# Two-block network on one core: the second block's projections in another order, its convolution without GpSimd

## The chip, the cores and the metric

One core of a Trainium2 chip runs the whole network in one program, everything in 32 bits. The figure is the device's time for the program in microseconds, the median of three runs.

## The reference

Two blocks follow each other on 256 tokens of 2048 channels, each two layers deep. The change is in the second block. It puts 16 learned tokens ahead (272 in all), normalizes, and runs this layer twice:

```
proj = h @ w_in                      # 2048 -> 5120 columns, nine segments
(c_val, c_glu, c_gate, q, k, v, a_gate, r_x, r_gate) = split(proj)

c = c_val * sigmoid(c_glu)                         # convolution branch, 512 channels
c = causal_depthwise_conv(c, conv_dw_w, conv_dw_b) # 31 taps
c = silu(layer_norm(c)) @ conv_pw_w + conv_pw_b
y_conv = c * silu(c_gate)

q, k = partial_rotary(q), partial_rotary(k)        # 16 query heads, 4 key heads of 64
y_attn = sliding_window_sink_attention(q, k, v, sinks) * silu(a_gate)

r = rg_lru(causal_depthwise_conv(r_x, lru_conv_w)) # recurrence over the tokens, 512 channels
y_lru = r * silu(r_gate)

h = layer_norm(alpha * h + concat(y_conv, y_attn, y_lru) @ w_out)
```

## The kernel before

**Weights stream past the operand.** Every product is done in three matmuls of half the precision each: a weight and the operand are split into a high part, a rounding, and a low part, the remainder. `weights` (L67) brings a half of a weight unit, 128x1024, by SP's DMA queue, ACT rounds it to `hi` (L76), and DVE subtracts to get `lo` (L78); there are three buffers for the raw half and four each for `hi` and `lo`. Such a half unit is the beat of the program: `wstat` (L103) does the 24 matmuls of a half unit (L119 to L121) into one of two sums in PSUM, `acc`, and then calls `tick` (L59). A projection of 512 columns is eight half units; its two sums are handed to an eviction at the end of half units six and eight.

**Side work is generators.** What is not a projection (attention, the convolution, the recurrence) is written as Python generators. `spawn` (L50) runs the first step of one, and every `tick` runs one step of each that is alive. This sets when the instructions are issued in the program, in half units. A planner then orders the instructions of each engine: it walks a model of the engines, takes what is ready, and among that what was issued first. `high_priority(offset=n)` makes instructions count as issued n instructions earlier, and a negative offset later: weights are 400 ahead, the convolution's taps 400 behind (`CONV_LATER`). The order of each engine is fixed in the program.

**A layer of block 2** (`layer`, L1093) does ten projections of the same normed operand `ht`: keys and values first, two of queries, then the convolution's value and gate, the recurrence's input, two gates of attention, the recurrence's gate and the convolution's gate. Then comes the pointwise product of the convolution (two half units, `pointwise`, L843), and four projections out of the four gated branches `ys`.

- The first projection runs before the layer norm of its operand is known. It is made of rows about a shift; `normed_acc` (L758) corrects it: the columns' mean part is scaled on ACT from `delta`, subtracted from PSUM on DVE (L766), multiplied by `rs` (L767), and shifted on ACT.
- `conv_branch` (L792) goes through 62 steps spread over 24 half units (`CONV_TICKS`). In each, DVE does one tap of a channel chunk (multiply and add, L790), and the side path does one of another chunk: ACT scales (L787), GpSimd adds (L788). Then come the layer norm over 512 channels, with sums on GpSimd and matmuls, and the split of the result, in eleven half units.
- `attend_kv` (L974) handles four heads that share keys, in 14 steps; the four of them start six half units apart.
- `lru_branch` (L865) does 16 taps on DVE with the same helper `tap` (L778), then gates, exponentials and a scan.
- `evict_k` and `evict_v` (L925, L937) rotate the keys, copy them for each head on GpSimd, and turn the values.
- In block 1, `layer_tables` (L174) loads constants and gains by GpSimd's DMA queue, pinned in the order of the program.

Of the kernel before, what the change touches and what calls it, by code (L numbers as in the profile page):

```python
# [35 lines left out]
class Net:  # L36
# [12 lines left out]
    # side work is a generator; the weight stream advances each by a step per half unit  # L49
# [32 lines left out]
    # tokens on the PSUM partitions: 512 columns of a weight, two token blocks  # L82
# [18 lines left out]
    # channels on the PSUM partitions: two subgroups of 256 columns. Where both parts of x fit  # L101
    # a bank, one matmul takes both, and the sums are added at the end
# [41 lines left out]
class Block1(Net):  # L144
# [29 lines left out]
    def layer_tables(self, l):  # L174
        nc, a, cp, cst = self.nc, self.a, self.tp, self.cst
        tabs = []
        load = lambda out, src: self.tc.keep_in_program_order(nc.gpsimd.dma_start(out=out, in_=src))
# [34 lines left out]
    # two channel chunks of x -> gained, split operand  # L212
# [185 lines left out]
    # two heads; st holds what the weight stream has brought  # L398
# [74 lines left out]
    # four heads  # L473
# [109 lines left out]
CONV_TICKS = 24  # L583
# [13 lines left out]
# columns of the per-channel parameters of a layer  # L597
CW, CB, CG, CBB, PB, LW, LB, BA, BX, LAM, PG, PBT, N_PC = 0, 124, 128, 132, 136, 140, 156, 160, 164, 168, 172, 188, 204
ROTC, ROTS, BAND, MCAUS, N_CST2 = 0, L2, 2 * L2, 2 * L2 + 416, 2 * L2 + 416 + 16
SHUFFLE = list(range(8, 16)) + list(range(0, 8)) + list(range(16, 32))  # L600


class Block2(Net):
# [18 lines left out]
    # layer norm over the channels, which lie on the partitions: sums about a shift. With gb, the  # L622
    # rows about the shift, times g, and g and b as two more columns, are an operand by themselves
# [112 lines left out]
    # the rows of hx, normed; their operand takes the place of the one about the shift, block by  # L736
    # block, when the first projection has read that
# [19 lines left out]
    # W g (x - shift) with W g and W b as further columns -> W applied to the normed rows  # L757
    def normed_acc(self, acc):  # L758
        nc = self.nc
        w = self.sm.tile([P, 2, 2], F32, tag="wgb", bufs=2, name="w")  # L760
        t = self.s2()
        with self.tc.high_priority(offset=GATE):
            nc.vector.tensor_copy(w, acc[:, :, L2 : L2 + 2])
            for c in range(2):
                nc.scalar.activation(t[:, c, :], self.delta, AF.Copy, scale=w[:, c, 0:1])
            nc.vector.tensor_tensor(out=t, in0=acc[:, :, :L2], in1=t, op=ALU.subtract)  # L766
        nc.vector.tensor_tensor(out=t, in0=t, in1=bc(self.rs, [P, 2, L2], 1), op=ALU.mult)  # L767
        for c in range(2):
            nc.scalar.activation(t[:, c, :], t[:, c, :], AF.Identity, bias=w[:, c, 1:2])
        return t  # L770
# [7 lines left out]
    def tap(self, pad, wbase, k, bias, out, c, j, side=False):  # L778
# [6 lines left out]
        elif side:  # L785
            t = self.cv.tile([P, L2], F32, tag="tap", bufs=4, name="tap")
            nc.scalar.activation(t, x, AF.Copy, scale=w)  # L787
            nc.gpsimd.tensor_tensor(out=o, in0=o, in1=t, op=ALU.add)  # L788
        else:
            nc.vector.scalar_tensor_tensor(out=o, in0=x, scalar=w, in1=o, op0=ALU.mult, op1=ALU.add)  # L790

    def conv_branch(self, cpad, res):  # L792
        nc = self.nc
        y = self.cv.tile([P, 4, L2], F32, tag="cv", name="y")
        for j in range(2 * TAPS):
            with self.tc.high_priority(offset=-CONV_LATER):
                self.tap(cpad, CW, TAPS, CB, y, j // TAPS, j % TAPS)
                self.tap(cpad, CW, TAPS, CB, y, 2 + j % 2, j // 2, side=True)
# [126 lines left out]
    def evict_k(self, acc):  # L925
        nc = self.nc
        t = self.normed_acc(acc)
# [8 lines left out]

    def evict_v(self, acc):  # L937
        nc = self.nc
        t = self.normed_acc(acc)
# [33 lines left out]
    # four heads that share keys  # L973
# [119 lines left out]
    def layer(self, l, gb_in):  # L1093
# [25 lines left out]
        wst(0, lambda sg, acc: self.spawn(self.evict_v(acc)) if sg else self.evict_k(acc), n=L2 + 2)  # L1119
        while norm in self.gens:  # L1120
            self.tick()
        self.spawn(self.decay())
        qq = self.Tp.tile([P, 2, 4, L2], F32, tag="T", name="qq")

        def attention():
# [278 lines left out]
```

## Time and profile before

| | |
|---|---|
| median of three runs | 3346.55 us |
| lowest, highest | 3342.49, 3347.16 us |
| span of the profiled execution | 3344.8 us |
| PE busy | 3272.3 us (98%) |
| DVE busy | 2204.3 us (66%) |
| ACT busy | 1653.2 us (49%) |
| GpSimd busy | 396.0 us (12%) |

PE is the matmul engine, PEld its load of weights, DVE the vector engine, ACT the scalar engine, POOL GpSimd, SP the engine whose queue issues the DMAs. The span goes from the first to the last instruction of one execution; it lies between the lowest and the highest of the three times. A busy PE is not PE at its peak, so the number of matmuls in a stretch says more than its busy time. Block 1 ends and block 2 begins at about 2490 us; its second layer begins at about 2915.

### The profile page before, as it was taken

How to read it: one execution, taken by the hardware profiler on the slowest of the kernel's cores; microseconds unless marked ns; L12 is line 12 of the kernel's file. 1: busy time of each engine (PE TensorE's matmuls, PEld its weight loads, DVE VectorE, ACT ScalarE, POOL GpSimd, SP SyncE). 2: the span in 40 equal slices, each digit the busy share in tenths (PEclk: the TensorE clock that was granted, in tenths of full speed). 3: DMA queues.
4: the chain of work that ended last, by engine and by line, in shares of the span. 5: the costliest groups of instructions: out<-in, count | busy, mean ns of one | idle time of the engine just before them, and what ended most of it. 6: DMA issues, size and time to landing. Idle time of an engine off the chain costs nothing.

```text
span 3344.8 us, 48525 instructions
## 1 busy us (share of the span) xinstructions
PE 3272.3 (98%) x19138; PEld 2878.7 (86%) x19138; DVE 2204.3 (66%) x2782; ACT 1653.2 (49%) x2308; POOL 396.0 (12%) x365
## 2 busy tenths in 40 slices
PE   8999999999999999999999999999999989999797
PEld 6888888888888888888888888888889989999797
DVE  7666655666665666666655666665687796776976
ACT  5444444444444454444544444444555565555653
POOL 2010100000000011110000000000032250322503
PEclk9999999999999999999999999999999999999899
DMA  6555555555555665555555555556654335453354
GB/s 217 173 170 171 172 188 188 179 176 175 174 172 187 205 212 185 171 175 169 170 193 188 178 174 174 174 176 195 199 169 155 102 125 170 158 164 103 115 181 134
DMA packets 164341, 573.05 MB, mean 171 GB/s; under 512 B 22464, under 2 KB 24768, under 8 KB 164112
## 3 DMA queue, kind: packets, MB, share of 16 engines
q1 hardware_dynamic: 163520, 567.72, 52.3%
q8 instruction: 150, 2.46, 0.3%
q0 software_dynamic: 592, 2.23, 0.2%
q14 instruction: 79, 0.65, 0.1%
HBM read 565.68 MB, written 4.19 MB: 170 GB/s over the span
## 4 chain that ended last, share of the span: by engine, by line
PE 90%; DVE 7%; issue 2%; DMA 1%; ACT 0%; POOL 0%; SPq 0%; DVEq 0%; POOLq 0%; ACTq 0%
PE acc L126 29%; PE acc L128 14%; PE acc L96 8%; PE acc L97 8%; PE acc L95 8%; PE acc L119 5%; PE acc L120 5%; PE acc L121 5%; DVE lo L78 2%; DVE y L790 2%; PE acc L125 1%; DVE x L790 1%; PE ps L343 1%; DMA raw<-wx 0%; PE ps L293 0%
## 5 line engine op out<-in xcount | busy, mean ns | idle before, releaser
L78 DVE TENSOR_TENSOR lo<-raw,hi 128x1024 fp32r<-128x1024 f32 x1060 | 1329.5, 1255 | 779.9 <-ACT hi L76 777.5
L76 ACT CAST hi<-raw 128x1024 fp32r<-128x1024 f32 x1060 | 1111.5, 1049 | 1230.6 <-PE acc L126 449.6
L126 PE MATMUL acc<-T,hi 128*128 128x512 f32 x4096 | 1439.9, 397 | 0.0
L128 PE MATMUL acc<-T,lo 128*128 128x256 f32 x3840 | 1077.7, 281 | 0.0
L126 PEld LDWEIGHTS acc<-T,hi 128*128 128x128 f32 x4096 | 762.0, 188 | 171.6
L128 PEld LDWEIGHTS acc<-T,lo 128*128 128x128 f32 x3840 | 725.8, 189 | 5.8
L119 PE MATMUL acc<-T,hi 128*128 128x272 f32 (+2 forms) x1792 | 531.1, 296 | 9.5 <-DVE t L1173 4.1
L95 PE MATMUL acc<-hi,T 128*128 128x512 f32 x1280 | 521.9, 408 | 8.6 <-ACT hi L76 8.6
L121 PE MATMUL acc<-T,lo 128*128 128x272 f32 (+2 forms) x1792 | 518.5, 289 | 2.8 <-DVE lo L78 2.8
L120 PE MATMUL acc<-T,hi 128*128 128x272 f32 (+2 forms) x1792 | 519.0, 290 | 0.9 <-POOL T L754 0.9
L96 PE MATMUL acc<-lo,T 128*128 128x512 f32 x1280 | 507.3, 396 | 3.0 <-DVE lo L78 3.0
L97 PE MATMUL acc<-hi,T 128*128 128x512 f32 x1280 | 507.0, 396 | 0.0
L119 PEld LDWEIGHTS acc<-T,hi 128*128 128x128 f32 x1792 | 344.7, 192 | 12.1 <-issue 8.0
L121 PEld LDWEIGHTS acc<-T,lo 128*128 128x128 f32 x1792 | 344.3, 192 | 3.4 <-DVE lo L78 3.4
L120 PEld LDWEIGHTS acc<-T,hi 128*128 128x128 f32 x1792 | 344.5, 192 | 2.9 <-POOL T L754 1.1
L95 PEld LDWEIGHTS acc<-hi,T 128*128 128x128 f32 x1280 | 241.6, 189 | 62.5 <-ACT hi L76 9.1
L96 PEld LDWEIGHTS acc<-lo,T 128*128 128x128 f32 x1280 | 242.3, 189 | 57.9 <-DVE lo L78 4.5
L97 PEld LDWEIGHTS acc<-hi,T 128*128 128x128 f32 x1280 | 241.3, 188 | 56.7
L133 ACT COPY sum<-acc 128x512 f32<-128x512 f32 x128 | 75.0, 586 | 222.1 <-PE acc L126 222.1
L134 DVE TENSOR_TENSOR sum<-acc,sum 128x512 f32<-128x512 f32 x128 | 88.5, 692 | 145.4 <-ACT sum L133 145.4
L788 POOL TENSOR_TENSOR y<-y,tap 128x272 f32<-128x272 f32 x120 | 123.4, 1065 | 248.7 <-ACT tap L787 129.7
L230 POOL TENSOR_TENSOR sqs<-sqs,sq 128x512 f32<-128x512 f32 x14 | 23.5, 1678 | 843.4 <-ACT sq L229 843.1
(326 smaller groups left out, 2413.8 us busy)
## 6 DMA issues: line engine op xcount, KB each, us to landing
raw<-ww SPq DMA_DIRECT2D x512, 512.0 KB, 4.3
raw<-wx SPq DMA_DIRECT2D x320, 512.0 KB, 3.8
raw<-w2in SPq DMA_DIRECT2D x160, 512.0 KB, 3.8
raw<-w2out SPq DMA_DIRECT2D x64, 512.0 KB, 4.2
x<-xT SPq DMA_DIRECT2D x8, 256.0 KB, 5.5
x<-xT SPq DMA_DIRECT2D x4, 512.0 KB, 5.9
x<-x SPq DMA_DIRECT2D x8, 256.0 KB, 3.0
x<-x SPq DMA_DIRECT2D x4, 512.0 KB, 5.1
```

Of the source, the lines that this page charges most:

```text
L76: nc.scalar.copy(hi, raw)
L78: nc.vector.tensor_tensor(out=lo, in0=raw, in1=hi.bitcast(F32), op=ALU.subtract)
L95: nc.tensor.matmul(o, xh, wh[:, k, :], start=first, stop=False)
L96: nc.tensor.matmul(o, xh, wl[:, k, :], start=False, stop=False)
L97: nc.tensor.matmul(o, xl, wh[:, k, :], start=False, stop=last)
L119: nc.tensor.matmul(o, wh[:, k, cs], xh, start=first, stop=False)
L120: nc.tensor.matmul(o, wh[:, k, cs], xl, start=False, stop=False)
L121: nc.tensor.matmul(o, wl[:, k, cs], xh, start=False, stop=last)
L126: nc.tensor.matmul(both, wh[:, k, cs], x[:, :, kc % 4, lo : lo + n], start=first, stop=last)
L128: nc.tensor.matmul(o, wl[:, k, cs], xh, start=False, stop=False)
L788: nc.gpsimd.tensor_tensor(out=o, in0=o, in1=t, op=ALU.add)
L790: nc.vector.scalar_tensor_tensor(out=o, in0=x, scalar=w, in1=o, op0=ALU.mult, op1=ALU.add)
```

## The change

Block 2's layer takes its projections in another order (the constants `CVAL` to `AGATE` give the place of each in `w2in`, which stays as it was), and the rows of `w2out` follow the new order of the branches. Value and gate of the convolution are first; then keys and values, half of the queries, the recurrence's input, the other half of the queries, the convolution's gate, the recurrence's gate, one gate of attention, the pointwise product, and the last gate of attention. The third and fourth part of attention wait until their queries are there (`there`).

The correction of the first projection is applied to the convolution's value. ACT first copies the sum out of PSUM, halved, and the correction is made on that copy and written into the convolution's input. Keys and values are copied by ACT without a correction.

The taps are spread over 44 half units. GpSimd has no part in them: ACT scales two channel chunks, and DVE adds both in one instruction (`tap_pair`), every second step. `gate` has a buffer of its own. The loads in `layer_tables` go by SP's queue and are no longer pinned, and the memory set aside for GpSimd's DMA is smaller.

```diff
-        load = lambda out, src: self.tc.keep_in_program_order(nc.gpsimd.dma_start(out=out, in_=src))
+        load = lambda out, src: nc.sync.dma_start(out=out, in_=src)
...
-CONV_TICKS = 24
+CONV_TICKS = 44
...
+CVAL, CGLU, KV, Q0, RX, CGATE, RGATE, AGATE = 3, 4, 0, 1, 5, 9, 8, 6
...
-    def normed_acc(self, acc):
+    def normed_acc(self, acc, out):
         nc = self.nc
         w = self.sm.tile([P, 2, 2], F32, tag="wgb", bufs=2, name="w")
         t = self.s2()
         with self.tc.high_priority(offset=GATE):
-            nc.vector.tensor_copy(w, acc[:, :, L2 : L2 + 2])
-            for c in range(2):
-                nc.scalar.activation(t[:, c, :], self.delta, AF.Copy, scale=w[:, c, 0:1])
-            nc.vector.tensor_tensor(out=t, in0=acc[:, :, :L2], in1=t, op=ALU.subtract)
+            nc.scalar.activation(t, acc[:, :, :L2], AF.Copy, scale=0.5)
+            nc.vector.tensor_scalar(w, acc[:, :, L2 : L2 + 2], 0.5, None, ALU.mult)
+        for c in range(2):
+            nc.vector.scalar_tensor_tensor(
+                out=t[:, c, :], in0=self.delta, scalar=w[:, c, 0:1], in1=t[:, c, :], op0=ALU.mult, op1=ALU.subtract)
         nc.vector.tensor_tensor(out=t, in0=t, in1=bc(self.rs, [P, 2, L2], 1), op=ALU.mult)
         for c in range(2):
-            nc.scalar.activation(t[:, c, :], t[:, c, :], AF.Identity, bias=w[:, c, 1:2])
-        return t
+            nc.scalar.activation(out[:, c, :], t[:, c, :], AF.Identity, scale=-1.0, bias=w[:, c, 1:2])
...
-        elif side:
-            t = self.cv.tile([P, L2], F32, tag="tap", bufs=4, name="tap")
-            nc.scalar.activation(t, x, AF.Copy, scale=w)
-            nc.gpsimd.tensor_tensor(out=o, in0=o, in1=t, op=ALU.add)
...
+    def tap_pair(self, pad, out, c, j):
+        nc = self.nc
+        t = out[:, c : c + 2, :] if j == 0 else self.cv.tile([P, 2, L2], F32, tag="tap", bufs=2, name="tap")
+        for i in range(2):
+            x, w = pad[:, c + i, j : j + L2], self.col(CW, (c + i) * TAPS + j)
+            if j == 0:
+                nc.scalar.activation(t[:, i, :], x, AF.Identity, scale=w, bias=self.col(CB, c + i))
+            else:
+                nc.scalar.activation(t[:, i, :], x, AF.Copy, scale=w)
+        if j:
+            o = out[:, c : c + 2, :]
+            nc.vector.tensor_tensor(out=o, in0=o, in1=t, op=ALU.add)
...
                 self.tap(cpad, CW, TAPS, CB, y, j // TAPS, j % TAPS)
-                self.tap(cpad, CW, TAPS, CB, y, 2 + j % 2, j // 2, side=True)
+                if j % 2 == 0:
+                    self.tap_pair(cpad, y, 2, j // 2)
...
-        t = self.normed_acc(acc)
+        t = self.taken(acc)
...
+    def taken(self, acc):
+        t = self.s2()
+        with self.tc.high_priority(offset=GATE):
+            self.nc.scalar.copy(t, acc[:, :, :L2])
+        return t
...
-        wst(0, lambda sg, acc: self.spawn(self.evict_v(acc)) if sg else self.evict_k(acc), n=L2 + 2)
+        cpad = self.cv.tile([P, 4, L2 + TAPS - 1], F32, tag="cpad", bufs=1, name="cpad")
...
+        wst(CVAL, lambda sg, acc: self.normed_acc(acc, c[:, 2 * sg : 2 * sg + 2, :]), n=L2 + 2)
         while norm in self.gens:
             self.tick()
...
+        wst(CGLU, ev)
+        self.spawn(self.conv_branch(cpad, cact))
         self.spawn(self.decay())
+        wst(KV, lambda sg, acc: self.spawn(self.evict_v(acc)) if sg else self.evict_k(acc))
...
+                while len(there) <= kv // 2:
+                    yield
...
+            wst(Q0 + cp, ev, lo)
+            there.append(cp)
+        query(0)
+        self.spawn(attention())
...
+        wst(RX, lambda sg, acc: nc.scalar.copy(rpad[:, 2 * sg : 2 * sg + 2, 3:], acc[:, :, :L2]))
         self.spawn(self.lru_branch(rpad, hlru))
+        query(1)
...
-        wst(6, gated(atts[0]), lo)
-        wst(7, gated(atts[1]), lo)
-        wst(8, gated(hlru), lo)
-        gate = self.lr.tile([P, 4, L2 + 3], F32, tag="rp", bufs=1, name="gate")
-        wst(9, lambda sg, acc: twice_silu(acc, gate[:, 2 * sg : 2 * sg + 2, lo:L2]), lo)
+        gate = self.lr.tile([P, 4, L2], F32, tag="gate", bufs=1, name="gate")
+        wst(CGATE, lambda sg, acc: twice_silu(acc, gate[:, 2 * sg : 2 * sg + 2, lo:]), lo)
+        wst(RGATE, gated(0, hlru), lo)
+        wst(AGATE, gated(2, atts[0]), lo)
         while not cact:
             self.tick()
-        ys.append(self.pointwise(a["pw"][l], cact, gate, lo))
+        ys[1] = self.pointwise(a["pw"][l], cact, gate, lo)
+        wst(AGATE + 1, gated(3, atts[1]), lo)
...
-    wo = np.concatenate([heads(wo[:, 512:1536], 1), wo[:, 1536:], wo[:, :512]], 1)
+    wo = np.concatenate([wo[:, 1536:], wo[:, :512], heads(wo[:, 512:1536], 1)], 1)
...
-    nc = bacc.Bacc("TRN2", target_bir_lowering=False, num_devices=1)
+    nc = bacc.Bacc("TRN2", target_bir_lowering=False, num_devices=1, dynamic_dma_scratch_size=1024)
```

## Rows read from the trace of the kernel before

Rows of stretches hold, in this order: the stretch in us; its length; busy time of PE, PEld, DVE, ACT and POOL, each with its number of instructions in brackets; the granted clock of the matmul engine as a share of the full one; the busy share of the DMA engines; GB/s. In rows in order of time, the bracket at the end is the idle time before the instruction and what ended it.

**Rows 1.** The profile's page: span, and engines' busy us, share, instructions:
```profile
span 3344.8 us, 48525 instructions
...
PE 3272.3 (98%) x19138; PEld 2878.7 (86%) x19138; DVE 2204.3 (66%) x2782; ACT 1653.2 (49%) x2308; POOL 396.0 (12%) x365
```

**Rows 2.** Stretches of 20 us in block 2:
```profile
2600.00:2620.00 20.00, 20.00 (x152) 18.90 (x151) 9.38 (x19) 11.23 (x27) 0.00 (x0) 1.00 0.38 123
2620.00:2640.00 20.00, 20.00 (x164) 18.87 (x164) 12.64 (x29) 8.72 (x13) 0.00 (x0) 1.00 0.32 106
...
2660.00:2680.00 20.00, 18.04 (x117) 17.24 (x115) 20.00 (x23) 13.31 (x25) 20.00 (x20) 0.83 0.24 79
2680.00:2700.00 20.00, 13.64 (x102) 12.82 (x102) 20.00 (x23) 14.71 (x29) 20.00 (x21) 0.89 0.17 55
2700.00:2720.00 20.00, 16.70 (x118) 15.51 (x117) 19.81 (x31) 10.08 (x21) 14.05 (x14) 0.85 0.33 107
2720.00:2740.00 20.00, 20.00 (x165) 19.24 (x165) 18.81 (x29) 13.35 (x17) 0.16 (x1) 1.00 0.50 160
...
2940.00:2960.00 20.00, 15.23 (x116) 14.80 (x115) 17.49 (x24) 11.27 (x20) 13.48 (x13) 0.91 0.49 159
...
3080.00:3100.00 20.00, 17.93 (x140) 17.05 (x138) 20.00 (x21) 14.00 (x26) 20.00 (x19) 1.00 0.24 79
3100.00:3120.00 20.00, 12.95 (x88) 12.34 (x88) 20.00 (x21) 14.34 (x28) 20.00 (x22) 0.89 0.22 72
3120.00:3140.00 20.00, 15.93 (x107) 15.25 (x108) 19.86 (x25) 11.71 (x23) 15.71 (x16) 0.77 0.26 87
3140.00:3160.00 20.00, 15.39 (x109) 15.00 (x107) 17.82 (x26) 8.72 (x12) 2.12 (x3) 0.83 0.49 159
```

**Rows 3.** DVE in order of time: start, us, line, operation:
```profile
2647.45 1.32 DVE L790 SCALAR_TENSOR_TENSOR y<-cpad,pc,y 128x272 f32<-128x272 f32 x3
2649.30 1.23 DVE L78 TENSOR_TENSOR lo<-raw,hi 128x1024 fp32r<-128x1024 f32 x1 [0.54 <-ACT hi L76]
...
2652.29 3.17 DVE L790 SCALAR_TENSOR_TENSOR y<-cpad,pc,y 128x272 f32<-128x272 f32 x4
2655.38 1.79 DVE L78 TENSOR_TENSOR lo<-raw,hi 128x1024 fp32r<-128x1024 f32 x1
```

**Rows 4.** POOL in order of time, same stretch:
```profile
2651.88 2.87 POOL L788 TENSOR_TENSOR y<-y,tap 128x272 f32<-128x272 f32 x3 [119.05 <-DVE ls L1008]
```

**Rows 5.** Groups from 2600 on: busy us, mean ns, idle before them:
```profile
L788 POOL TENSOR_TENSOR y<-y,tap 128x272 f32<-128x272 f32 x120 | 123.4, 1065 | 248.7 <-ACT tap L787 129.7 <-DVE ls L1008 119.1
L790 DVE SCALAR_TENSOR_TENSOR y<-cpad,pc,y 128x272 f32<-128x272 f32 x120 | 89.9, 792 | 0.4
L787 ACT ACTIVATE tap<-cpad,pc 128x272 f32<-128x272 f32 x120 | 58.9, 519 | 26.4 <-POOL y L788 26.2
...
L909 DVE TENSOR_TENSOR_SCAN hl<-g,x 128x544 f32<-128x544 f32 x4 | 5.2, 1290 | 0.1
L903 ACT ACT_TABLE_LOAD x4 | 5.1, 1283 | 0.1
...
L934 POOL COPY kz<-t 64x272 f32<-64x272 f32 x4 | 3.1, 775 | 0.2
...
L892 DVE TENSOR_TENSOR x<-g,x 128x544 f32<-128x544 f32 x4 | 2.9, 716 | 0.1
```

**Rows 6.** Waits of PE from 2880 to 2980: us in total, times, longest:
```profile
PE acc L119 <- DVE t L766: 3.5, 1, 3.5
```

**Rows 7.** Two stretches of 10 us at the start:
```profile
30.00:40.00 10.00, 7.12 (x21) 5.27 (x20) 8.53 (x13) 4.69 (x6) 2.61 (x2) 0.66 0.61 194
40.00:50.00 10.00, 10.00 (x48) 8.26 (x49) 9.16 (x16) 5.41 (x8) 0.96 (x2) 1.00 0.58 193
...
cst<-cst POOLq DMA_DIRECT2D x1, 833.0 KB, 4.8
```

**Rows 8.** DVE in order of time at block 2's start:
```profile
2492.32 1.32 DVE L969 TENSOR_SCALAR m<-pc 128x4 f32<-128x4 f32 x1
```

More of the change, by code (lines that the diff above doesn't have):

```diff
@@ L776, in col, with tap @@
         return self.pc[:, base + i : base + i + n]
-    def tap(self, pad, wbase, k, bias, out, c, j, side=False):
+    def tap(self, pad, wbase, k, bias, out, c, j):
         nc = self.nc
@@ L935, in evict_k @@
             nc.gpsimd.tensor_copy(self.kz[r, kv, :M], k[r, kv // 2, 256:])
+    def taken(self, acc):
[3 more added lines that the diff above has]
+        return t
     def evict_v(self, acc):
         nc = self.nc
-        t = self.normed_acc(acc)
+        t = self.taken(acc)
         for _ in range(V_SLACK):
@@ L1118, in layer, with ev @@
         norm = self.spawn(self.normed(gb_in, ht))
-        wst(0, lambda sg, acc: self.spawn(self.evict_v(acc)) if sg else self.evict_k(acc), n=L2 + 2)
+        cpad = self.cv.tile([P, 4, L2 + TAPS - 1], F32, tag="cpad", bufs=1, name="cpad")
+        nc.vector.memset(cpad[:, :, : TAPS - 1], 0.0)
+        c = cpad[:, :, TAPS - 1 :]
+        wst(CVAL, lambda sg, acc: self.normed_acc(acc, c[:, 2 * sg : 2 * sg + 2, :]), n=L2 + 2)
         while norm in self.gens:
             self.tick()
+        def ev(sg, acc):
+            t = self.s2()
+            nc.scalar.activation(t, acc[:, :, :L2], AF.Tanh, scale=0.5)
+            o = c[:, 2 * sg : 2 * sg + 2, :]
+            nc.vector.scalar_tensor_tensor(out=o, in0=t, scalar=1.0, in1=o, op0=ALU.add, op1=ALU.mult)
+        wst(CGLU, ev)
+        self.spawn(self.conv_branch(cpad, cact))
         self.spawn(self.decay())
+        wst(KV, lambda sg, acc: self.spawn(self.evict_v(acc)) if sg else self.evict_k(acc))
         qq = self.Tp.tile([P, 2, 4, L2], F32, tag="T", name="qq")
+        there = []
         def attention():
@@ L1143, in finish, with query, ev @@
             yield from self.attend_end(cp, qq[:, cp], osb, atts[cp], not last)
-        for cp in range(2):
-            def ev(sg, acc, q=qq[:, cp]):
+        def query(cp):
+            def ev(sg, acc):
                 t = self.s2()[:, :, lo:]
                 nc.scalar.activation(t, acc[:, :, :n], AF.Copy, scale=0.125)
-                self.rotary(q[:, 2 * sg : 2 * sg + 2, lo:], t)
-            wst(1 + cp, ev, lo)
-            if cp == 0:
-                self.spawn(attention())
-        cpad = self.cv.tile([P, 4, L2 + TAPS - 1], F32, tag="cpad", bufs=1, name="cpad")
-        nc.vector.memset(cpad[:, :, : TAPS - 1], 0.0)
-        c = cpad[:, :, TAPS - 1 :]
-        wst(3, lambda sg, acc: nc.scalar.activation(c[:, 2 * sg : 2 * sg + 2, :], acc[:, :, :L2], AF.Copy, scale=0.5))
-        def ev(sg, acc):
-            t = self.s2()
-            nc.scalar.activation(t, acc[:, :, :L2], AF.Tanh, scale=0.5)
-            o = c[:, 2 * sg : 2 * sg + 2, :]
-            nc.vector.scalar_tensor_tensor(out=o, in0=t, scalar=1.0, in1=o, op0=ALU.add, op1=ALU.mult)
-        wst(4, ev)
-        self.spawn(self.conv_branch(cpad, cact))
+                self.rotary(qq[:, cp, 2 * sg : 2 * sg + 2, lo:], t)
+            wst(Q0 + cp, ev, lo)
+            there.append(cp)
+        query(0)
+        self.spawn(attention())
         rpad = self.lr.tile([P, 4, L2 + 3], F32, tag="rp", bufs=1, name="rpad")
         nc.vector.memset(rpad[:, :, :3], 0.0)
-        wst(5, lambda sg, acc: nc.scalar.copy(rpad[:, 2 * sg : 2 * sg + 2, 3:], acc[:, :, :L2]))
+        wst(RX, lambda sg, acc: nc.scalar.copy(rpad[:, 2 * sg : 2 * sg + 2, 3:], acc[:, :, :L2]))
         self.spawn(self.lru_branch(rpad, hlru))
-        ys = []
+        query(1)
+        ys = [None] * 4
         def twice_silu(acc, out):
@@ L1173, in twice_silu, with gated @@
                 nc.vector.scalar_tensor_tensor(out=out, in0=out, scalar=1.0, in1=acc[:, :, :n], op0=ALU.add, op1=ALU.mult)
-        def gated(src):
+        def gated(i, src):
             def ev(sg, acc):
@@ L1179, in ev @@
                 if sg == 0:
-                    ys.append(self.tt())
-                y = ys[-1]
+                    ys[i] = self.tt()
+                y = ys[i]
                 sl = slice(2 * sg, 2 * sg + 2)
```

## Prediction

> **What bounds the kernel now.** I read the page's table of engines first, then the profiled execution cut into stretches of 20 us, then the places where the matmul engine loses time, on each engine in order of time. The table [rows 1] shows PE busy for 98% of the span, so nearly all of the time is matmul work that the change leaves alone; what can be won is what PE loses. The stretches say where. PE handles 152 to 165 matmuls in a full stretch of block 2 (the lower figure beside attention), but only 117, 102 and 118 in the three from 2660 on, and 140, 88, 107 and 109 in the four from 3080 on, with the granted clock at 0.77 to 0.89 in six of the seven, so partly at the lower, 1.2 GHz, of its two levels [rows 2]. Those are the two stretches in which the taps of the convolution run, one for each layer. DVE is busy for 20.00 of 20 us in most of them, and POOL with it. Much of DVE's time there is waste: three taps take 1.32 us, 0.44 each, and a weight split 1.23; from 2651.88 on POOL adds taps too [rows 4], and the next four DVE taps take 3.17 us, 0.79 each, the next split 1.79 [rows 3]. Since every weight half must pass DVE before PE can use it, a slow DVE there is a slow PE.
>
> **What the 2660 and 3080 stretches cost.** 337 matmuls in 60 us: at 165 in 20 us they need 40.8, at 152 they need 44.3. Lost: 15.7 to 19.2, taken 17. 444 matmuls in 80 us: 53.8 to 58.4 are needed. Lost: 21.6 to 26.2, taken 24. Together 41, bounds 37 to 45.
>
> **The change part by part.**
>
> *POOL leaves the taps.* In each layer 60 POOL adds of 1065 ns go [rows 5]. With them goes the slowing of DVE: its 60 following taps, now 792 ns in the mean [rows 5], should take the 0.44 us of the undisturbed rows [rows 3]; so should the 16 taps of the recurrence in each layer. The splits fall back from 1.79 to 1.23. What comes instead: 30 DVE adds for each layer, over two channel chunks, 128x544 with both inputs in SBUF. The nearest row is a product of that shape, 716 ns [rows 5]. Convolution on DVE is then 62 x 0.44 + 30 x 0.716 = 27.3 + 21.5 = 48.8 us for a layer, against 45 now (89.9 us for two layers). So DVE's work doesn't shrink on this account, but neither do its other instructions suffer. ACT's taps go from 60 to 62 instructions of 519 ns, which is nothing: ACT is busy 10 to 15 us in 20 there [rows 2].
>
> *The taps start at half unit 16 and not at 40, spread over 44 half units.* Counting the steps of the generators: value and gate take half units 0 to 15; taps are issued in 16 to 59; attention's four parts start at 34, 40, 49 and 55; the recurrence runs from 40 to 58. Does DVE hold all that? Beside attention DVE is busy 9.38 to 12.64 of 20 us with splits and attention [rows 2]. At 152 matmuls in 20 us the 24 weight matmuls of a half unit are 3.2 us; with attention's own, an estimate of one in seven, a half unit is 3.7, so 44 are some 163 us and convolution adds 48.8 / 163 x 20 = 6.0 in 20. The recurrence is 16 x 0.44 = 7.0 plus 13.5 us (eight groups of rows, L887 to L909, of which the first row of 716 ns and the last of 1290 ns are shown [rows 5]), 20.5 us over 18 half units of about 4 us: 5.7 in 20. The sum is 21.1 to 24.3 of 20 where all three meet, 18 half units or 72 us: a backlog of 4 to 15 us at the worst. Outside that, 15.4 to 18.6 of 20. The backlog has where to go: the taps are queued 400 places later than they are issued, they are issued until half unit 59, and behind them 11 half units are set aside for sums, matmuls and tables whose work is far shorter than that. I take 3.5 us lost in each layer, 7 in all; the bounds are 0 and 15 for each, 30.
>
> *The order of the units.* Matmuls, their sizes and the weights loaded are the same in number; only their order changes, and that of the output weight's rows with them. Two things are late next: the pointwise product stands at half unit 72 and its operand is due at 71, one spare where there were five (75 and 80); and the last gate stands behind it, whose attention is due at 78 and needed at 79. Both are inside the 7 us above. The gate has its own buffer, so it waits for no buffer of the recurrence: no cost, since PE shows no wait there now.
>
> *First eviction raw.* At the start of layer 1 PE waited 3.5 us for a bank that a DVE subtraction (L766) had to read, queued behind the rotation of the keys [rows 6]; the stretch handled 116 matmuls, so 14.1 us of work at 165, 5.9 lost [rows 2]. After the change ACT copies the bank at once and the rotation comes two units later. I take 4 back, bounds 0 to 5.9. At layer 0's start PE waits for other things, so nothing.
>
> *Loads of the tables from SP instead of POOL.* Eight loads, among them one of 833 KB [rows 7], join the queue of the weights and lose the order they were pinned to; behind each stand the weight halves. PE handled 21 matmuls in 30 to 40 us and 48 in the next 10 [rows 7]: 5.6 us lost just after these loads now. It could vanish, or come back at another point as the loads stand ahead of weights; I take 0, bounds a gain of 5.6 and a loss of 5.6.
> The Trainium skill's page "DMA: Bandwidth & Descriptors", section "Issuing engines are not separate DMA queues", says that transfers issued by any engine share the same 16 DMA engines and that another issuer saves only issue time. By that rule the bytes delay the weights as much as before and the term is 0; by the row alone it could be 5.6 of gain. No run here shows it yet.
>
> *Tables of ACT.* The decay's logarithm may now come after the gate's tanh, which could add two loads of a table in each layer, 1283 ns each [rows 5]: 5.1 us of ACT in all, hidden while ACT has 5 to 10 us free in 20.
>
> *What POOL keeps.* The keys' copies stay on POOL, eight in a layer, the larger 775 ns [rows 5], and now run beside taps: at most 6.2 us in a layer in which DVE's taps may take double, so 3 us more of DVE, in a stretch with room. It is inside the bound of 15.
> The Trainium skill's page "SBUF — State Buffer", section "Who interferes with whom", says that a DVE instruction with two inputs in SBUF and a GpSimd instruction that reads SBUF shut each other out for a whole instruction. That speaks against this change as far as POOL is not emptied: the new pair adds have two such inputs too. By it each of the eight copies stops DVE for its whole length, 6.2 us in a layer and not 3, and the sum would be 6 us smaller at most. For the taps the trace agrees (0.79 us beside POOL, 0.44 alone) [rows 3, 4]; the pair adds no row shows yet.
>
> **The sum.** 41 + 4 - 7 + 0 = 38 us. From the span of 3344.8 that gives 3306.8; the median of the three runs is 1.75 us above this span, so the time is 3346.55 - 38, about 3309.
>
> **The rivals.**
> *DVE stays the bound beside attention.* The backlog is at its upper end and isn't absorbed: 15 us in each layer, and PE waits at the pointwise product. 41 + 4 - 30 = 15 won: 3332. For it: the sum of 21 to 24 in 20. Against it: durations in the rows overlap by some 0.08 us each, so the sum is too high, and 13 half units of slack follow.
> *ACT's queue stops (the other side).* Each pair of scaled taps needs one of two buffers, given back by a DVE add of the lowest rank. If DVE lags by more than two pairs, about three half units or 11 us, ACT stands at a tap and the next cast of weights stands behind it, and with it PE. With a lag of 15 us that would be 4 us for each of some 12 pairs in the dense 18 half units: 48 for a layer, 96 in all, less some 6 us covered by weight buffers in each layer; 96 - 12 = 84, less the 45 won, is 39 lost: 3386. It decides from a lag of 11 us. For it: ACT does stand in front of taps now, 26.2 us in all, waiting for POOL [rows 5]. Against it: the dense stretch begins when half the taps are done.
> *The spread doesn't hold.* The order is made by a planner that lets ready work float ahead: the decay's first DVE instruction ran at 2492.32 [rows 8], before the projection was over after which it is issued. The taps may then fill DVE solidly in the units of keys and first queries, where, by the stretches beside attention, 7 to 11 us in 20 are free [rows 2], and be done early. DVE's sum is the same and the dense stretch lighter: 3306 to 3309, so this shares the forecast's time.
>
> **How the numbers follow.** The forecast, with or without the spread: 0.76. DVE stays the bound: 0.13, most of it still faster. ACT's queue stops: 0.07. Neither way visible, gains eaten by the start and the buffers: 0.04. A measurement of this kernel tells about 0.2%, 6.7 us. Faster by more than that: 0.76 + 0.10 = 0.86; the same: 0.06; slower: 0.08. The range: the best sum is 45 + 5.9 + 5.6 - 0 = 56, 3290, which needs every bound at once; I go to 3294. The upper end takes in the first rival with its own loss at the start, 3332 + 5.6: 3337.
>
> **What would show it.** Right: the taps on DVE take about 0.44 us and their pair adds about 0.7; no stretch of 20 us in block 2 with fewer than 140 matmuls other than at the layers' ends; POOL idle there. Wrong: taps still at 0.8 without POOL; a wait of PE for the convolution's operand ahead of the pointwise product; ACT idle behind tap buffers; DVE at 20 of 20 for longer than 80 us with PE below 150.

## The result, and the profile after

| | before | after |
|---|---|---|
| median | 3346.52 us (four runs) | 3305.61 us (four runs, 3305.16 to 3306.15) |
| span of the profiled execution | 3344.8 us | 3304.2 us |
| PE busy | 3272.3 us (98%) | 3256.1 us (99%) |
| DVE busy | 2204.3 us (66%) | 2181.8 us (66%) |
| GpSimd busy | 396.0 us (12%) | 269.0 us (8%) |

The ratio after to before is 0.9881, 95% interval 0.9867 to 0.9895: 41 us faster. The forecast was 3309, within 3294 to 3337.

The page of the kernel after, the lines that answer to [rows 1]:

```profile
span 3304.2 us, 48363 instructions
...
PE 3256.1 (99%) x19138; PEld 2865.2 (87%) x19138; DVE 2181.8 (66%) x2842; ACT 1651.3 (50%) x2308; POOL 269.0 (8%) x237
```

Stretches of 20 us of the kernel after, with the columns of [rows 2]:

```profile
2560.00:2580.00 20.00, 20.00 (x161) 20.00 (x160) 20.00 (x34) 14.91 (x27) 6.22 (x8) 1.00 0.57 177
...
2620.00:2640.00 20.00, 20.00 (x147) 18.88 (x146) 19.97 (x45) 11.35 (x28) 0.00 (x0) 1.00 0.44 139
2640.00:2660.00 20.00, 20.00 (x154) 19.23 (x153) 18.12 (x38) 14.40 (x31) 0.00 (x0) 1.00 0.39 120
2660.00:2680.00 20.00, 20.00 (x142) 18.31 (x141) 14.90 (x27) 11.68 (x17) 0.95 (x1) 1.00 0.34 105
...
3040.00:3060.00 20.00, 17.84 (x134) 16.31 (x133) 19.48 (x44) 14.96 (x38) 0.00 (x0) 1.00 0.40 123
3060.00:3080.00 20.00, 20.00 (x154) 18.69 (x153) 17.76 (x29) 13.02 (x19) 2.86 (x2) 1.00 0.36 114
3080.00:3100.00 20.00, 20.00 (x158) 19.34 (x158) 15.27 (x31) 14.64 (x29) 1.08 (x1) 1.00 0.42 127
```

The stretches with 88 to 118 matmuls and a granted clock of 0.77 to 0.89 [rows 2] are gone; PE is at 20.00 of 20 in all but one of these, and the clock at 1.00 in all. DVE is as full as before, 20.00 of 20 from 2560 on, and PE doesn't suffer from it. The groups of the convolution after, from 2480 on, with the columns of [rows 5]:

```profile
L789 DVE SCALAR_TENSOR_TENSOR y<-cpad,pc,y 128x272 f32<-128x272 f32 x120 | 58.2, 501 | 0.2
L800 ACT ACTIVATE tap<-cpad,pc 128x272 f32<-128x272 f32 x120 | 55.7, 515 | 25.5 <-DVE y L803 24.4 <-ACT hi L76 0.3
L803 DVE TENSOR_TENSOR y<-y,tap 128x544 f32<-128x544 f32 x60 | 43.1, 718 | 0.5 <-ACT tap L800 0.4
```

A DVE tap takes 501 ns instead of 792 [rows 5], a pair addition 718.

Where the 41 us were won is read from landmarks, the first table activation of each layer norm (L709 before, L711 after): 2495 and 2497 us at the start of block 2, 2917 and 2901 at the end of its first layer, 3328 and 3287 at the end of the second. The start of the program lost 2 us, the first layer won 18, the second 25.

### The profile page after: what moved, and what is told of

It reads as the page before. It is cut to its first block, busy times and chain, and to the rows that moved or that the text cites. A ratio compares the mean times of both kernels' runs of the same rounds, so it can differ in the third digit from the quotient of the medians.

```text
span 3304.2 us, 48363 instructions
## 1 busy us (share of the span) xinstructions
PE 3256.1 (99%) x19138; PEld 2865.2 (87%) x19138; DVE 2181.8 (66%) x2842; ACT 1651.3 (50%) x2308; POOL 269.0 (8%) x237
## 4 chain that ended last, share of the span: by engine, by line
PE 92%; DVE 3%; issue 2%; ACT 1%; DMA 1%; POOL 1%; SPq 0%; DVEq 0%; ACTq 0%; POOLq 0%
PE acc L126 29%; PE acc L128 14%; PE acc L97 8%; PE acc L96 8%; PE acc L95 8%; PE acc L119 6%; PE acc L120 6%; PE acc L121 6%; DVE lo L78 1%; PE acc L125 1%; DMA raw<-wx 1%; PE ps L343 1%; PE ps L293 0%; PE ps L307 0%; PE ps L1007 0%
## 5 line engine op out<-in xcount | busy, mean ns | idle before, releaser
L119 PE MATMUL acc<-T,hi 128*128 128x272 f32 (+2 forms) x1792 | 524.9, 293 | 3.8 <-ACT T L755 2.4
L120 PE MATMUL acc<-T,hi 128*128 128x272 f32 (+2 forms) x1792 | 513.9, 287 | 1.4 <-POOL T L756 1.4
```

Of the source, the lines that this page charges most:

```text
L119: nc.tensor.matmul(o, wh[:, k, cs], xh, start=first, stop=False)
L120: nc.tensor.matmul(o, wh[:, k, cs], xl, start=False, stop=False)
```

## The experiments

Twelve kernels, in three groups. The kernel before ran beside each group: 3346.32, 3347.11 and 3345.73 us.

### GpSimd put back into the new order

```diff
-                if j % 2 == 0:
-                    self.tap_pair(cpad, y, 2, j // 2)
+                self.tap_side(cpad, y, 2 + j % 2, j // 2)
```
Here `tap_side` is the side path of before: ACT scales, GpSimd adds.

> The changed kernel with the old side path of the taps: ACT scales one chunk, GpSimd adds it, two channel chunks on each side; order of the units, 44 half units and the raw eviction stay. Theory A (GpSimd's adds slow DVE, and that was the loss): DVE's taps go back to about 0.8 us, weight splits beside them to 1.8, PE loses 15 to 40 us again somewhere in the taps' stretches: 3320 to 3345. Theory B (what counts is that the taps have 44 half units beside attention, GpSimd or not): the slower DVE is absorbed, 3303 to 3312.

Measured: 3358.30 us, 1.0035 of the time before (1.0022 to 1.0048). That is 53 us more than after, and beyond both expectations. Three stretches of its first layer:

```profile
2560.00:2580.00 20.00, 12.65 (x82) 11.96 (x81) 20.00 (x23) 13.31 (x23) 20.00 (x20) 0.86 0.26 80
2580.00:2600.00 20.00, 16.29 (x109) 15.59 (x109) 17.85 (x22) 10.28 (x19) 19.74 (x23) 0.88 0.33 106
2600.00:2620.00 20.00, 13.97 (x92) 12.87 (x91) 19.82 (x24) 12.19 (x20) 16.94 (x16) 0.91 0.32 105
```

DVE gets 23 instructions through in 20 us where it does 34 after, and PE 82 matmuls for 161. The new order by itself, with GpSimd's path, is slower than the kernel before: unless GpSimd leaves, the change wins nothing. Whether it was GpSimd's reads or the chain of sums through it, this run doesn't tell.

### The new tap path in the old order

```diff
-                self.tap(cpad, CW, TAPS, CB, y, 2 + j % 2, j // 2, side=True)
+                if j % 2 == 0:
+                    self.tap_pair(cpad, y, 2, j // 2)
```

> The kernel before with one edit: the side path of the taps is the pair of ACT scalings and one DVE add; order, 24 half units, first eviction and loads as before. Theory A: DVE's taps at 0.44 to 0.50 us, no slowed splits, PE's loss in the two stretches falls from 41 us to 5 to 20, since 48.8 us of DVE work still fall into 24 half units beside the recurrence: 3310 to 3325. Theory B: without the longer stretch DVE is as overfull as before: 3335 to 3350.

Measured: 3325.38 us, ratio 0.9937 (0.9922 to 0.9952): 21 us, half of the gain, between the two expectations. The costliest waits of PE in block 2 (us in total, times, longest):

```profile
PE ps L823 <- POOL t L620: 8.6, 2, 4.4
PE ps L837 <- POOL t L620: 5.2, 2, 4.3
```

L823 and L837 are the matmuls that take the mean and the variance of the convolution's result over the channels. PE works in a fixed order, and these stand in it; here it reached them before the sum of all taps was there. The taps (at 0.50 us) ran until 2758 and 3166, the matmul came at 2762 and 3170. In the taps' stretches ahead of that, from 2640 to 2740 and from 3060 to 3160, PE handles 155 to 170 matmuls in 20 us, so the loss of the kernel before is gone there; these waits are new. The matmul of the mean in the kernel before (L809), with its idle time at the end:

```profile
L809 PE MATMUL ps<-t,o 128*128 128x272 f32 x4 | 1.2, 392 | 0.0
```

It runs at 2770 and 3193 us there, and its input is ready at 2745 and 3162.

### The new kernel with 24 half units

```diff
-CONV_TICKS = 44
+CONV_TICKS = 24
```

> The changed kernel with the taps issued over 24 half units and not 44. If the planner floats taps forward wherever DVE is free, the number is idle: 3303 to 3309, taps at the same places as with 44. If the spread itself carries the gain (theory B): taps bunch, DVE is overfull from half unit 16 to 40, 3315 to 3330.

Measured: 3325.77 us, ratio 0.9937 (0.992 to 0.9954), 20 us slower than after. Yet the taps run at the same time in both: the 72 multiply-and-add taps of DVE in the first layer (60 of the convolution, 12 of the recurrence) from 2545 to 2649 us with 24 half units, from 2543 to 2647 with 44. What differs is where the two matmuls stand. Waits of PE in block 2 with 24 half units:

```profile
PE ps L823 <- POOL t L622: 5.2, 2, 3.3
PE ps L837 <- POOL t L622: 2.7, 2, 1.8
```

GpSimd's sum and PE's matmul with 24 half units, in order of time:

```profile
2654.15 1.35 POOL L818 TENSOR_TENSOR t<-y 128x544 f32<-128x544 f32 x1 [77.48 <-DVE y L803]
2655.59 1.62 POOL L622 TENSOR_TENSOR t<-t 128x272 f32<-128x272 f32 x1
2657.26 0.73 PE L823 MATMUL ps<-t,o 128*128 128x272 f32 x2 [1.96 <-POOL t L622]
```

Four stretches of 20 us with 24 half units:

```profile
2640.00:2660.00 20.00, 18.04 (x130) 16.72 (x130) 16.15 (x27) 13.94 (x37) 2.97 (x2) 1.00 0.35 107
2660.00:2680.00 20.00, 16.10 (x99) 14.54 (x99) 13.64 (x24) 10.26 (x14) 2.95 (x2) 0.83 0.17 54
...
3060.00:3080.00 20.00, 16.06 (x110) 14.63 (x109) 14.65 (x27) 13.36 (x28) 4.01 (x3) 0.84 0.36 119
3080.00:3100.00 20.00, 19.11 (x123) 17.37 (x123) 15.30 (x30) 10.15 (x13) 1.37 (x2) 0.82 0.16 54
```

With 44 half units the same matmul runs at 2734 and 3135 us and waits for nothing. With 24 PE is there before the sum and idles, and the granted clock falls to 0.83 in the first layer and to 0.84 and 0.82 in the second, so partly to the lower, 1.2 GHz, level: weight matmuls start 0.23 us apart and not 0.13 from 2667 to 2670, 0.21 and not 0.12 from 3079 to 3087. From 2640 to 2680 PE handles 130 + 99 matmuls where after does 154 + 142, and from 3060 to 3100 110 + 123 for 154 + 158: 146 fewer, at 160 in 20 us some 18 us. That is nearly all of the loss. The two matmuls' waits are 7.9 us of it; the rest is the lower clock and a few shorter waits beside them, such as 2.1 us for ACT's copy of a sum of the queries (L1183).

### The loads on SP, in the kernel before

```diff
-        load = lambda out, src: self.tc.keep_in_program_order(nc.gpsimd.dma_start(out=out, in_=src))
+        load = lambda out, src: nc.sync.dma_start(out=out, in_=src)
```

> The kernel before with one edit: the eight loads of tables and gains by SP's queue, not pinned. From the two traces (matmuls in the first 60 us: 203 before, 186 after; block 2 begins 2 us later after the change): 2 to 4 us slower, 3349 to 3351, all of it in the first 60 us. The rival, that the loads gave part of the gain: 3341 to 3344.

Measured: 3348.79 us, ratio 1.0008 (0.9998 to 1.0017), some 2.5 us more than the kernel before beside it; the interval just takes in no difference. The trace shows it at the start: PE handles 451 matmuls in the first 120 us, 464 before, and the first L141 on DVE comes at 135 us instead of 132. The kernel after is like this one (450, 135). The 203 and 186 of the expectation are sums over shorter stretches, in which a matmul on a border counts twice; the first 60 us taken as one have 195 and 181.

### The first eviction from PSUM again, in the new order

```diff
-            nc.scalar.activation(t, acc[:, :, :L2], AF.Copy, scale=0.5)
-            nc.vector.tensor_scalar(w, acc[:, :, L2 : L2 + 2], 0.5, None, ALU.mult)
+            nc.vector.tensor_copy(w, acc[:, :, L2 : L2 + 2])
+            for c in range(2):
+                nc.scalar.activation(t[:, c, :], self.delta, AF.Copy, scale=w[:, c, 0:1])
+            nc.vector.tensor_tensor(out=t, in0=acc[:, :, :L2], in1=t, op=ALU.subtract)
```

> The changed kernel, but the first projection's eviction of a layer keeps its two sums in PSUM until they are corrected, as before the change: no raw copy by ACT, the subtraction reads the bank. Theory A (the raw eviction is worth the 4 us that the sum gave it): 3308 to 3311, PE waiting 3 us or more in one piece for a bank read by DVE at the start of layer 1. Theory B (in the new order the first two units' eviction has nothing ahead of it on DVE, so the raw copy buys nothing): 3303 to 3307, no such wait.

Measured: 3304.42 us, ratio 0.9876 (0.9861 to 0.9891): no loss without the raw copy. PE's wait at the start of the second layer is 2.1 us for this subtraction (L769), against 1.4 for a multiplication (L767) after and 3.5 [rows 6] before. What shortened it is the order: before, DVE rotates keys from 2943.25 to 2946.62 us ahead of the second subtraction; now the convolution's value is evicted first, and only a weight split stands ahead of it.

### Four buffers for ACT's taps

```diff
-... self.cv.tile([P, 2, L2], F32, tag="tap", bufs=2, name="tap")
+... self.cv.tile([P, 2, L2], F32, tag="tap", bufs=4, name="tap")
```

> The changed kernel with four buffers instead of two for ACT's scaled taps. ACT stood 24.4 us in all behind these buffers in the changed kernel. Theory A (those waits are hidden, PE has weights enough): 3304 to 3307, ACT's wait before its taps down to less than half, PE's matmuls by stretch the same. Theory B (the waits hold up casts and with them PE, in the one stretch from 3040 with 134 matmuls above all): 3300 to 3303, and that stretch above 145.

Measured: 3304.41 us, ratio 0.9874 (0.986 to 0.9889), no more than 1.2 us from after. ACT's group of taps in this kernel:

```profile
L800 ACT ACTIVATE tap<-cpad,pc 128x272 f32<-128x272 f32 x120 | 55.2, 515 | 24.4 <-DVE y L803 23.7
```

The wait behind the buffers stayed at 23.7 us, where less than half was expected; with either depth ACT stands as long behind DVE's additions. It costs nothing either way, as ACT is busy for 8 to 16 of 20 us there after.

### GpSimd busy, with nothing depending on it

```diff
+        idle = self.cv.tile([P, 2, L2], F32, tag="idle", bufs=1, name="idle")
+        nc.vector.memset(idle, 0.0)
         for j in range(2 * TAPS):
             with self.tc.high_priority(offset=-CONV_LATER):
+                nc.gpsimd.tensor_tensor(out=idle[:, 0, :], in0=idle[:, 0, :], in1=idle[:, 1, :], op=ALU.add)
```

> The changed kernel with 62 idle additions on GpSimd in each layer, 128x272 of two inputs from an own buffer that nothing else reads, issued with the taps: GpSimd's work of old beside DVE, without any dependence of DVE or ACT on it. Theory A (what GpSimd costs is that both engines get in each other's way while it reads): DVE's taps at 0.75 to 0.85 us while it runs, against 0.50, casts late, 3330 to 3358. Theory B (the 53 us of the run with GpSimd's old path came from the chain through GpSimd's sums and ACT's buffers behind them): taps at 0.50 and 3304 to 3312.

Measured: 3378.21 us, ratio 1.0094 (1.0078 to 1.0109). Much of it isn't what was to be measured, as PE's waits show:

```profile
PE acc L120 <- POOL T L756: 42.5, 3, 39.5
PE acc L121 <- DVE lo L78: 13.6, 13, 2.0
```

The additions need only one fill of their own buffer, so the planner put those of both layers at the start of block 2, from 2489 to 2649 us, and 56 of them stood in GpSimd's fixed order ahead of the first low part of the normed operand (L756), for which PE stopped. DVE stood too, 39.7 us ahead of the second layer's fill of that buffer (L809). The rest, 72.6 - 42.5 = 30 us, would be one layer's slowing. One thing can be read all the same: from 2600 to 2640 us, beside these additions on a buffer of their own, a split takes 1768 ns, a tap 1007 and a pair addition 1285, where after it is 1210, 487 and 712. The next but one run puts the additions where the taps are.

### GpSimd writing only

```diff
+        idle = self.cv.tile([P, 4, L2], F32, tag="idle", bufs=1, name="idle")
         for j in range(2 * TAPS):
             with self.tc.high_priority(offset=-CONV_LATER):
+                nc.gpsimd.memset(idle, 0.0)
```

> The changed kernel with 62 GpSimd fills of a 128x1088 buffer in each layer, issued with the taps: GpSimd busy beside DVE, but writing only. Theory A (any GpSimd work beside DVE slows it): taps of DVE at 0.75 us or more and 3325 to 3358. Theory B (only a GpSimd instruction that reads stands in the way of a DVE instruction with two inputs): taps at 0.50 us, 3304 to 3309. The Trainium skill's page SBUF — State Buffer, section Who interferes with whom, states B.

Measured: 3312.18 us, ratio 0.9897 (0.9881 to 0.9914), 6.6 us more than after and 3 beyond the second expectation; one wait of PE for L756 behind these fills is 6.2 us, where it is 1.4 after. GpSimd fills for 18 to 19 of 20 us from 2540 to 2640, and DVE, from 2560 to 2600, goes on as after: split 1238 ns in both, taps 517 (after 509), pair additions 741 (716).

### GpSimd reading, beginning with the taps

```diff
+        idle = self.cv.tile([P, L2], F32, tag="idle", bufs=1, name="idle")
         for j in range(2 * TAPS):
             with self.tc.high_priority(offset=-CONV_LATER):
+                nc.gpsimd.tensor_tensor(out=idle, in0=cpad[:, 0, j // 2 : j // 2 + L2],
+                                        in1=cpad[:, 1, j // 2 : j // 2 + L2], op=ALU.add)
```

> The changed kernel with 62 additions on GpSimd in each layer that read two chunks of the convolution's input and write a buffer nobody reads; they can't begin before the taps can, which the idle additions of the earlier run did (those stood in GpSimd's queue in front of the normed operand, and PE waited 42.5 us for that). Theory A (GpSimd's reads slow DVE): taps at 0.75 to 1.0 us and pair additions at 1.0 to 1.3 us while GpSimd adds, 3325 to 3358, about what the old GpSimd path cost in the new order (53 us) or somewhat less. Theory B (that path's cost was the chain of sums through GpSimd): 3304 to 3312.

Measured: 3359.39 us, ratio 1.0039 (1.0024 to 1.0054), the same as with GpSimd's old path (1.0035), though nobody waits for these sums. DVE's groups from 2560 to 2600 us, first of this kernel, then of the kernel after:

```profile
L78 DVE TENSOR_TENSOR lo<-raw,hi 128x1024 fp32r<-128x1024 f32 x9 | 15.0, 1669 | 0.0
L803 DVE TENSOR_TENSOR y<-y,tap 128x544 f32<-128x544 f32 x11 | 13.0, 1185 | 0.0
L789 DVE SCALAR_TENSOR_TENSOR y<-cpad,pc,y 128x272 f32<-128x272 f32 x13 | 11.3, 871 | 0.0
```

```profile
L78 DVE TENSOR_TENSOR lo<-raw,hi 128x1024 fp32r<-128x1024 f32 x13 | 16.1, 1238 | 0.0
L789 DVE SCALAR_TENSOR_TENSOR y<-cpad,pc,y 128x272 f32<-128x272 f32 x20 | 10.0, 509 | 0.0
L803 DVE TENSOR_TENSOR y<-y,tap 128x544 f32<-128x544 f32 x13 | 9.3, 716 | 0.0
```

And in order of time, GpSimd of this kernel (seven additions in a row), then its DVE beside them:

```profile
2577.09 8.05 POOL L811 TENSOR_TENSOR idle<-cpad 128x272 f32<-128x272 f32 x7
```

```profile
2578.36 1.68 DVE L78 TENSOR_TENSOR lo<-raw,hi 128x1024 fp32r<-128x1024 f32 x1
...
2579.97 0.46 DVE L935 STREAM_SHUFFLE t<-t 128x272 f32<-128x272 f32 x1
...
2580.70 1.19 DVE L938 TENSOR_TENSOR t<-t,cst 128x544 f32<-128x544 f32 x1
```

DVE's instructions with two tensors to read are 35 to 71% longer beside them; the shuffle, which reads one, takes its 0.46 us as in the kernel after. PE pays at the splits:

```profile
PE acc L121 <- DVE lo L78: 28.6, 21, 2.6
```

So in the new order it is the reading at the same time, and not the chain through GpSimd, that costs the 53 us. Nor is it that both read the same tile: the additions on a buffer of their own, above, slowed DVE as much. For the kernel before, the same slowing is in its rows (taps of 792 ns [rows 5]); how much the chain added there was not tried.

### The old order with four half units more

```diff
-CONV_TICKS = 24
+CONV_TICKS = 28
```
(in the kernel of the second experiment)

> The kernel before with the pair path on ACT and DVE and CONV_TICKS at 28: the old order of the units, the matmul of the convolution's mean four half units later, as late as that order has room for. Theory A (what the old order lacks is only room between the last tap and that matmul, for which PE waited 13.8 us): 3308 to 3318. Theory B (the old order keeps a loss of its own, since taps begin too late for any spread): 3322 to 3328.

Measured: 3311.43 us, ratio 0.9896 (0.988 to 0.9913). The matmul of the mean stands four half units later, and the wait for it is nearly gone:

```profile
PE acc L119 <- DVE t L766: 3.5, 1, 3.5
PE ps L823 <- POOL t L620: 2.5, 1, 2.5
```

Four half units are worth 14 us, and the old order reaches all but 6 of the 41. The stretches say the same: 160 + 158 matmuls from 2740 to 2780, where the run with 24 had 138 + 120, and 133 + 155 from 3160 to 3200 where it had 67 + 163; 118 more, at 160 in 20 us some 15 us.

### The new order with 34 half units

```diff
-CONV_TICKS = 44
+CONV_TICKS = 34
```

> The changed kernel with CONV_TICKS at 34, halfway between 24 (20 us slower) and 44. Theory A (a threshold: the number only places PE's matmul of the mean, some ten half units earlier, near 2697 and 3098 us, where its input, ready at about 2657 and 3081, is there already): 3304 to 3308. Theory B (gradual: fewer half units crowd DVE): 3312 to 3320.

Measured: 3306.52 us, ratio 0.9882 (0.9867 to 0.9896), as with 44. The matmul of the mean runs at 2689 and 3091 us, its input is summed from 2659 and 3071 on; no wait. So the number works by a threshold, which in the new order lies between 24 and 34.

### Three places as before, together

The changed kernel with the eviction from PSUM, four tap buffers, and the loads of the tables from GpSimd's queue in order; the diffs are those above, the one of the loads reversed.

> The changed kernel with the first eviction from PSUM as before, four buffers for ACT's taps, and the tables loaded from GpSimd in order as before: the three places where the runs so far gave the old form no disadvantage. If the 2.5 us that the move of the loads cost in the kernel before are to be had back here, 3300 to 3303; if that cost belonged to the old kernel alone, 3303 to 3306.

Measured: 3299.64 us (3299.22 to 3300.17), ratio 0.9861 (0.9846 to 0.9876), some 6 us below after, the fastest of all, and just below the lower expectation. At the start and in the one stretch after in which PE waited, in this kernel:

```profile
30.00:40.00 10.00, 7.12 (x34) 5.40 (x34) 8.73 (x13) 5.08 (x8) 2.60 (x2) 1.00 0.57 205
40.00:50.00 10.00, 10.00 (x47) 8.16 (x46) 8.74 (x15) 6.11 (x9) 0.96 (x2) 1.00 0.56 194
...
3040.00:3060.00 20.00, 20.00 (x158) 19.05 (x157) 19.00 (x40) 14.69 (x36) 0.00 (x0) 1.00 0.34 114
```

By landmarks (L711 at 2495, 2898 and 3281; after 2497, 2901 and 3287), 2 us come at the start, 1 in the first layer and 3 in the second. In the second the wait for L899 is gone, which also goes with the eviction alone (156 matmuls in that stretch) and not with the buffers alone (137). Why an eviction at 2920 moves a wait at 3048 wasn't tried; the planner's order of ACT differs.

## Why the prediction was right, and where not

**GpSimd leaves the taps: right, and now shown.** The prediction took 0.44 us for a DVE tap and 0.716 for a pair addition; they take 0.501 and 0.718 us (0.44 was a third of a row of three that overlap; after, one starts 0.41 us after another, so this is the same speed). Its convolution on DVE, 48.8 us a layer, is 58.2 / 2 + 43.1 / 2 = 50.7, or 51.4 with the two first taps. Its mechanism, that GpSimd's additions slow DVE and a slow DVE slows PE, holds, in the new order, against the rival that the chain through GpSimd was the cost: idle additions cost what the real ones did, 1.0039 against 1.0035.

**From DVE to PE: another way than by the splits.** The prediction says that a slow DVE is a slow PE because every weight half must pass DVE. With GpSimd's path in the new order PE did wait for splits, 32.2 us. In the kernel before it hardly did. Two waits of its PE (us in total, times, longest, from 2600 on), then DVE ahead of the one of 6.4 us that ends at 2699:

```profile
PE ps L1043 <- DVE osb L1033: 16.5, 3, 9.4
PE acc L121 <- DVE lo L78: 2.8, 3, 1.3
```

```profile
2693.97 4.66 DVE L790 SCALAR_TENSOR_TENSOR y<-cpad,pc,y 128x272 f32<-128x272 f32 x5
2698.55 0.74 DVE L1033 TENSOR_TENSOR osb<-ps,ls 128x256 f32<-128x256 f32 x2
```

In the two tap stretches PE's waits are 29.4 us: 16.5 for attention's output (L1033), which stood on DVE behind slowed taps, 7.4 for other work on DVE (L1057, L1173), 5.0 for a copy of attention's on ACT, and 0.5 for splits. So the weights were in time, and PE stopped for other results that DVE had late; what the lower clock cost comes on top.

The Trainium skill's page "SBUF — State Buffer", section "Who interferes with whom", says that DVE instructions with two inputs in SBUF are held up by a GpSimd instruction that reads SBUF, and not by one that only writes. The traces agree on both: a pair addition takes 1185 ns beside reads, 741 beside fills and 716 alone. That each shuts the other out for a whole instruction, which the prediction takes from the same section, the traces don't show: in 10.3 us from 2576.27 of the run with idle reads GpSimd does nine additions, 0.83 us each where DVE is idle, and DVE eight two-input instructions that take 6.4 us after; one by one that would be 13.8. For the keys' copies beside the taps this made 6.2 us of DVE, and the prediction took 3; in the first layer after, the instructions beside 6.4 us of copies are 0.6 us longer in all (two splits of 1.30 and 1.43 us for 1.23, two taps of 0.73 and 0.64 for 0.50).

**41 us from the two tap stretches: the sum right, the next limit missing.** The new tap path alone, in the old order, filled both stretches, and yet brought only 21 us. Most of the other 20 was lost at a step that the prediction doesn't have: the matmuls of the convolution's mean and variance stand in PE's fixed order, CONV_TICKS half units and a few after the first tap, and PE stops at them if DVE isn't through. In the kernel before, PE was late enough itself and waited for neither; a faster PE does. With 24 half units this costs 14 us in the old order and 20 in the new one. The prediction looked for room ahead of the pointwise product, at half unit 72, and found one half unit of spare; the narrow place was earlier. It counted the 44 half units only as room on DVE; that they also keep PE clear of this wait is luck as far as the prediction goes. With 28 half units the old order comes within 6 us of the new one with 44: that much is left for the order of the units, the first eviction and the loads together.

**The spread over 44 half units: taps right, conclusion wrong.** The rival "the spread doesn't hold" said that the planner would let the taps run early and that the time would be the same. The first half happened: the taps of the first layer run from about 2543 to 2648 us with 24, 34 and 44 half units alike. From this follows that the number moves no tap. That it moves nothing does not follow: what it moves is the matmul that waits for the last one.

**The residual of 7 us: too large.** DVE was at 20.00 of 20 for 80 us as feared, PE at 147 to 170 matmuls there. Of the tap stretches only the one from 3040 lost, 134 matmuls for 158, 3 us; by its 134 it misses the sign that no stretch inside a layer falls below 140. The keys' copies on GpSimd, 6.22 us beside taps from 2560 on, cost no matmul in that stretch (161).

**First eviction raw, 4 us: mis-sized.** The wait fell from 3.5 to 1.4 us, but without the raw copy it is 2.1 and the time no worse. The old order kept the 3.5 us in both runs with the new tap path. So the order won it, and the raw copy is worth nothing that these runs can tell.

**Loads from SP, 0: some 2 us lost.** By the run of the kernel before with this one edit, and by its reversal in the last run, it is 2 to 3 us, inside the bounds of ±5.6. The trace after shows where: the squares on which the first norm rests are done on ACT at 38.76 us, three together, behind the casts, and PE waits for their sum; before they were at 21.38, 29.59 and 31.04. The two costliest waits of PE in the first 120 us after:

```profile
PE acc L95 <- ACT hi L76: 8.4, 1, 8.4
PE ps L237 <- POOL sqs L230: 6.5, 1, 6.5
```

Before, the second didn't exist, and PE waited 3.0 us for DVE's splits, where it is 0.7 after. Why the planner put the squares later when the loads changed their queue is not settled.
The Trainium skill's page "DMA: Bandwidth & Descriptors", section "Issuing engines are not separate DMA queues", gave 0 for this term, as all queues share the 16 DMA engines. The runs show 2 to 3 us, and the trace puts them down to the order of the work, not to the transfers, so they say nothing against the rule.

**Tables of ACT.** 17 loads in block 2 before and 17 after: none came on top.

**The rivals.** "DVE stays the bound" (3332) did not happen, though its condition did: the backlog was absorbed, since PE's first need of the last tap (L823) comes 60 to 80 us after it. "ACT's queue stops" (3386) fell too: ACT did stand behind the tap buffers, 24.4 us, and neither doubling them nor the 91.1 us of waits in the run with idle reads shows PE waiting for a cast in that place.

**By layers.** Predicted 17 - 3.5 = 13.5 for the first and 24 + 4 - 3.5 = 24.5 for the second; they gave 18 and 25, and the start took 2: 41 in place of 38.

## What to carry to other kernels

GpSimd next to a busy DVE is not a free helper: where both read, give its work to ACT and DVE even if DVE's own count of instructions rises, and look at the durations of DVE's instructions, not its busy share, to see it. When side work is spread over a weight stream, find the first instruction of the in-order engine that consumes its end; the spread only has to be long enough for that instruction to come late, and more brings nothing (here 34 half units did as well as 44). When a slow engine is sped up, look for what the in-order engine will reach sooner: a place where it waited for nothing can be its next wait. Work that depends on nothing floats to the front of its queue and can stop what stands behind it.

## What the runs showed of the hardware that was not expected

124 idle additions of 1.0 us on GpSimd cost the kernel 53.8 us (3359.39 against 3305.61), nearly half of their own length, without any dependence. In the run with 24 half units in the new order, waits of PE of 1.8 to 3.3 us were followed by matmuls at the lower clock (0.82 to 0.84 of the full one granted in three stretches of 20 us), and the 20 us lost are more than double the 7.9 us of waits at the two matmuls. The length of the wait alone doesn't tell: the first of these, of 1.96 us, was followed by matmuls 0.13 us apart, and the stretch with the 2.5 us wait of the old order with 28 half units has a granted clock of 1.00; in the kernel before, a wait of 1.96 us that ends at 2667.91 was followed by 7 us at 0.52.
